# One layer of a hybrid SSM and convolution block: how the last product of the down projection gets its operands, and where the odd rows are normalised

## The chip, the core and the metric

The kernel runs on one core of a Trainium2 chip. The metric is device time in microseconds (us) for one execution; the median of three runs is given. A profile of one more execution shows each instruction of the five engines: PE (TensorE), DVE (VectorE), ACT (ScalarE), POOL (GpSimd) and SP (SyncE, which here only issues DMAs).

## What is computed

The layer takes x of 1024 rows by 1024 columns. A token-mixing half (SSM branch, short convolution, gates, output projection, LayerNorm) gives a new x. The part that matters here is the end:

```python
hid = jax.nn.silu(jnp.einsum('bsd,df->bsf', x, w_gate)) * jnp.einsum('bsd,df->bsf', x, w_up)
ffn = jnp.einsum('bsf,fd->bsd', hid, w_down)
x = layer_norm(ALPHA * x + ffn, ln2_g, ln2_b)
```

`hid` has 2816 columns, `w_down` is 2816 by 1024, and all is float32.

## The kernel before, in words

Each large product is done by Strassen's scheme: seven products of half-size matrices in place of eight. Each fp32 operand is split into a high part (rounded to `fp32r`) and a low part (what is left), and a product is three matmuls: low by high, high by low, high by high (L1480 to L1482). ACT makes the high part by a copy; DVE makes the low part by a subtraction (both through line L115, the helper `sub`).

There are two ways to split. `split` has ACT write the high part to SBUF once, and DVE subtract that from the raw tile: both inputs of DVE lie in SBUF. `psplit` has ACT write the high part twice, first to one of two PSUM banks (`hp`), then to SBUF, and DVE subtracts the PSUM copy: one input of DVE is in SBUF and one in PSUM.

The down projection runs the seven products in the order 2, 6, 3, 1, 4, 7, 5 (`ORD_E`), each in 11 steps over the inner dimension (`kp` 0 to 10), so that step n of 0 to 76 is a product and a kp: product 4 is steps 44 to 54, product 7 is steps 55 to 65, product 5, the last, is steps 66 to 76. In a usual step PE does 12 matmuls of 128 by 512 (four row blocks `tp`, three matmuls each). In the last product only `tp` 0 (and `tp` 1, three steps behind, `LAG`) run inside the steps: 3 matmuls in steps 66 to 68, then 6. After step 76 come the 9 matmuls left of `tp` 1, the 33 of `tp` 2, and 66 matmuls of 128 by 256 for `tp` 3 (L1561 to L1563).

The order of the instructions is the order in which the loop over n emits them (each engine works its own queue in that order). In step n the loop emits:

- at the first step of a product, DVE's additions of the previous product's row blocks 2 and 3 from PSUM into `acc` (`e_evac`, L112 or L1470),
- the loads for step n+8 (SP), and POOL's operand sum for step n+6 (`tB`, L106; only for products whose right operand is a sum of two blocks, so none for product 5),
- the splits for step n+3 (`e_split`): left operand A (`rAh`, `rAl`) and right operand B (`rBh`, `rBl`); in product 5 only B is left to do here, because A was split early,
- `e_early`: in the steps of the table `EARLY`, the A operand of one kp of product 5, by `psplit`; its load is issued six steps earlier,
- one stage of the generator `odd_tiles`, when it is due,
- the matmuls, and at the last step of a product the additions of row blocks 0 and 1.

`acc` holds eight row tiles. The four odd ones (`acc[:, 4 + tp]`) get their last addition from product 4, so they can be normalised while products 7 and 5 run. `odd_tiles` does that: for each of four tiles the statistics on DVE (`bn_stats` L990, `bn_aggr` L991), then one inverse square root for all four by small DVE instructions (`ln_rstd`, `ln_bias`, twelve instructions, the last at L1013), then for each half and tile `ln_half`, and the store. `ln_half` has two forms: with `engs = None` it is two DVE instructions (L1020, L1021), otherwise one activation on ACT (L1023) and a multiplication and an addition on POOL (L109, L112). The four even tiles follow after product 5: `finish` for tiles 0 to 2 (statistics on DVE, then ACT and POOL), and the last tile wholly on DVE.

Of the kernel before, what the change touches and what calls it, by code (L numbers as in the profile page):

```python
# [47 lines left out]
def kernel(  # L48
# [22 lines left out]
    V, S, G, PE = nc.vector, nc.scalar, nc.gpsimd, nc.tensor  # L71
# [52 lines left out]
    def half(h):  # L124
        return slice(512 * h, 512 * h + 512)
# [203 lines left out]
    def start(gen, s=0):  # L329
        bg.append([gen, s])  # L330
# [656 lines left out]
    def ln_stats(t, tmp_pool, mv, nm):  # L987
        stt = tmp_pool.tile([P, 2, 6], F32, tag="bst6", name=f"bn{nm}", bufs=2)
        for h in range(2):
            V.bn_stats(stt[:, h], t[:, half(h)])  # L990
        V.bn_aggr(mv, stt)  # L991

    def ln_rstd(tmp_pool, mv, n, nm):
        var = mv[:, :, 1]
        w = tmp_pool.tile([P, 5, n], F32, tag=f"lnw{n}", name=f"lnw{nm}", bufs=2)
        v, a, r, r1, b = (w[:, i] for i in range(5))
        ts(v, var, EPS, -0.5, ALU.add, ALU.mult)
        it = tmp_pool.tile([P, n], I32, tag=f"iti{n}", name=f"it{nm}", bufs=2)
        ts(it, v.bitcast(I32), -0.5, 519526879.0, ALU.mult, ALU.add)
        r0 = it.bitcast(F32)  # L1000
        for ri in (r, r1, r):
            if n == 1:
                ts(a, r0, r0, v, ALU.mult, ALU.mult)
                ts(ri, a, 1.5, r0, ALU.add, ALU.mult)
            else:
                mul(a, r0, r0)
                mul(a, a, v)
                V.scalar_tensor_tensor(ri, a, 1.5, r0, ALU.add, ALU.mult)
            r0 = ri
        return r, b  # L1010

    def ln_bias(mv, r, b):
        V.scalar_tensor_tensor(b, mv[:, :, 0], -1.0, r, ALU.mult, ALU.mult)  # L1013

    def ln_half(t, lg, mean, r, b, h, engs):
        ln_cols(t, lg, mean, r, b, half(h), engs)
# [228 lines left out]
    NK = NF // 2  # L1245
# [15 lines left out]
    def load_a(m, kp):  # L1261
        if (m, kp) not in as_:
            t = as_[m, kp] = e1a["p"].tile([P, 512], F32, tag="As", name=f"As{m}_{kp}", bufs=12)
            nc.sync.dma_start(t, a_d[m - 1, kp])
# [119 lines left out]
    def e_load(n):  # L1384
        if n < len(seq):
            m, kp = seq[n]
            if m != 5:
                load_a(m, kp)
            op = XOP[m]
            for ij in op if len(op) == 1 else op[1:]:  # L1390
                ld(kp, *ij)

    def e_add(n):
        if n < len(seq):
            m, kp = seq[n]
            op = XOP[m]
            if len(op) == 1:
                pend[n] = ld(kp, *op[0])
            else:
                pend[n] = e1.tile([P, 512], F32, tag="tB", name=f"tB{n}", bufs=4)  # L1400
                tt(pend[n], ld(kp, *op[1]), ld(kp, *op[2]), OPS[op[0]], G)

    def place(m, kp, kind):
        if m != 5:
            return (e1, f"r{kind}h", 4), (e1, f"r{kind}l", 4)
        if kind == "B":
            return (e1, f"Bx_{kp}", 1), ((e1, f"own{kp}", 1) if kp < 7 else (e1, "rBl", 4))
        if kp < 5:
            return tuple((e1a["p"], f"B00_{2 * kp + r}", 1) for r in range(2))
        return tuple((e1, f"own{2 * kp - 3 + r}", 1) for r in range(2))  # L1410

    def split_op(m, kp, kind, src):
        th, tl = place(m, kp, kind)
        h = th[0].tile([P, 512], F32R, tag=th[1], name=f"r{kind}h{m}_{kp}", bufs=th[2])
        l = tl[0].tile([P, 512], F32R, tag=tl[1], name=f"r{kind}l{m}_{kp}", bufs=tl[2])
        (split if m == 2 or (m == 5 and kind == "B") else psplit)(h, l, src)
        return [h, l]

    def e_split(n):
        if n < len(seq):  # L1420
            m, kp = seq[n]
            a = early.pop(kp) if m == 5 else split_op(m, kp, "A", as_.pop((m, kp)))
            ring[n] = a + split_op(m, kp, "B", pend.pop(n))

    early = {}
    EARLY = {40 + 2 * i: kp for i, kp in enumerate((5, 6, 7, 8, 9, 10, 0, 1, 2, 3, 4))}

    def e_early(n):
        if n + 6 in EARLY:
            load_a(5, EARLY[n + 6])  # L1430
        if n in EARLY:
            early[EARLY[n]] = split_op(5, EARLY[n], "A", as_.pop((5, EARLY[n])))

# [12 lines left out]
    def open_e2():  # L1446
        close(epi_cm)
        close(wring_cm)
        e2["cm"], e2["p"] = opened("e2")
        acc = e2["p"].tile([P, 8, D], F32, tag="acc", name="acc")  # L1450
        return acc, e2["p"].tile([P, 2, D], F32, tag="lg", name="lg2")
# [14 lines left out]
    def e_evac(m, tp):  # L1466
        for par, h, f in UPD[m]:
            t = acc[:, 4 * par + tp, half(h)]
            if (m, par, h) in ((2, 1, 0), (2, 1, 1), (3, 0, 1), (1, 0, 0)):
                V.scalar_tensor_tensor(t, t, ALPHA, eb[m, tp], ALU.mult, ALU.subtract if f is sub else ALU.add)  # L1470
            else:
                f(t, t, eb[m, tp])

    def e_mm(m, kp, tp, r):
        ah, al, bh, bl = r
        if kp == 0:
            eb[m, tp] = bank(f"pe{m}_{tp}")
        ps = eb[m, tp]
        c = slice(tp * P, (tp + 1) * P)
        PE.matmul(ps, al[:, c], bh, start=kp == 0, stop=False)  # L1480
        PE.matmul(ps, ah[:, c], bl, start=False, stop=False)  # L1481
        PE.matmul(ps, ah[:, c], bh, start=False, stop=kp == NK - 1)  # L1482

    def odd_tiles():
        mv = e2["p"].tile([P, 4, 2], F32, tag="mv4", name="mv4")
        for tp in range(4):
            ln_stats(acc[:, 4 + tp], e2["p"], mv[:, tp], f"o{tp}")
            yield 2
        r, b = ln_rstd(e2["p"], mv, 4, "o")
        ln_bias(mv, r, b)  # L1490
        yield 1
        for h in range(2):
            for tp in range(4):
                J = 4 + tp
                engs = None if h == 0 and tp < 3 else (G, G)
                ln_half(acc[:, J], lg2, mv[:, tp, 0:1], r[:, tp : tp + 1], b[:, tp : tp + 1], h, engs)
                nc.sync.dma_start(out[:, J, half(h)], acc[:, J, half(h)])
                yield 1

    LAG = 3  # L1500
    for n in range(len(seq)):
        m, kp = seq[n]
        if n == NFIRST:
            acc, lg2 = open_e2()
        if kp == 0 and n:
            for tp in (2, 3):
                e_evac(seq[n - 1][0], tp)
        e_load(n + 8)
        e_add(n + 6)
        e_split(n + 3)  # L1510
        if NFIRST <= n < NFIRST + 4:
            nc.sync.dma_start(acc[:, n - NFIRST + 4], x1_d[n - NFIRST + 4])
        if 14 <= n < 18:
            nc.sync.dma_start(acc[:, n - 14], x1_d[n - 14])
        if n == 20:
            nc.sync.dma_start(lg2, ln[:, 2:4])
        e_early(n)
        if n == 5 * NK + 3:
            start(odd_tiles(), n)
        for it in list(bg):  # L1520
            if it[1] <= n:
                try:
                    it[1] = n + next(it[0])
                except StopIteration:
                    bg.remove(it)
        if m == 5:
            e_mm(m, kp, 0, ring[n])
            if kp >= LAG:
                e_mm(m, kp - LAG, 1, ring[n - LAG])
        elif kp > 1 or n < 2:  # L1530
            for tp in range(4):
                e_mm(m, kp, tp, ring[n])
        else:
            for tp in range(2):
                e_mm(m, kp, tp, ring[n])
            if kp == 1:
                for k in range(2):
                    for tp in range(2, 4):
                        e_mm(m, k, tp, ring[n - 1 + k])
        if m != 5 and kp != 0:  # L1540
            ring.pop(n)
            if kp == 1:
                ring.pop(n - 1)
        if kp == NK - 1 and m != 5:
            for tp in range(2):
                e_evac(m, tp)
# [112 lines left out]
```

## Time and profile before

| | us |
|---|---|
| median of 3 runs | 1295.02 (1293.82 to 1295.74) |
| the profiled execution | 1294.12 |
| its span, first to last instruction | 1292.3 |
| PE busy in the span | 1207.6 (93%) |
| DVE busy | 860.5 (67%) |
| POOL busy | 783.4 (61%) |
| ACT busy | 737.0 (57%) |

The profiled execution lasted 1.8 us longer than its span and was 0.9 us below the median. All times below are us from the start of the span. A row of a timeline reads: start, duration, engine, line, operation, output<-inputs, shapes, count, and in brackets how long the engine sat idle before it and what released it. Durations overlap a little where an engine pipelines, so the pace of a queue is read from start to start. PEclk is the share of TensorE's full clock that was granted.

### The profile page before, as it was taken

To read this page: it belongs to the slowest core of one execution; us is meant where nothing else is said; L and a number is where in the kernel's file an instruction comes from. 1 tells how busy PE (TensorE), PEld (TensorE's weight loads), DVE (VectorE), ACT (ScalarE), POOL (GpSimd) and SP (SyncE) were. 2 spreads that over 40 slices of the span, in tenths; PEclk is the share of its full clock that TensorE was granted. 3 is DMA by queue.
4 is the path that set the end of the run, shared out by engine and by line. 5 is a ranking of instruction groups with operands and counts; after the bars stand their busy time and mean duration, and the time that the engine had idled before them with its cause. 6 is when DMAs were issued, how large, how long until landed. Compare 5 with 4: busy or idle time off the path is not lost. (4 is left out here: it accounts for less than half of the span.)

```text
span 1292.3 us, 16665 instructions
## 1 busy us (share of the span) xinstructions
PE 1207.6 (93%) x5365; PEld 981.3 (76%) x5365; DVE 860.5 (67%) x1319; ACT 737.0 (57%) x1288; POOL 783.4 (61%) x579
## 2 busy tenths in 40 slices
PE   7789899989899999999869999999999999999976
PEld 4577677777677888888757888888888887888756
DVE  6998688786676675688984444444344467667797
ACT  5645776778776252243433555555555555878841
POOL 4836878796862125123688777778778764544444
PEclk9989999999999999999989999999999999999988
DMA  5221343344446645224204423323222419845212
GB/s 198 74 94 46 103 117 97 116 153 144 141 140 223 204 139 199 79 98 147 98 33 145 165 82 114 106 91 122 107 98 98 155 66 348 296 135 171 70 54 77
DMA packets 88023, 166.07 MB, mean 129 GB/s; under 512 B 17792, under 2 KB 27008, under 8 KB 87680
## 3 DMA queue, kind: packets, MB, share of 16 engines
q1 hardware_dynamic: 87936, 165.00, 38.2%
q8 instruction: 43, 0.70, 0.2%
q14 instruction: 44, 0.36, 0.1%
HBM read 114.77 MB, written 44.83 MB: 123 GB/s over the span
## 5 line engine op out<-in xcount | busy, mean ns | idle before, releaser
L180 PE MATMUL ps_f<-x1h,wl_f 128*128 128x512 f32 x616 | 242.5, 394 | 13.1 <-DVE wl_f L115 9.5
L181 PE MATMUL ps_f<-x1l,wh_f 128*128 128x512 f32 x616 | 241.6, 392 | 2.8 <-DVE x1l L115 2.8
L182 PE MATMUL ps_f<-x1h,wh_f 128*128 128x512 f32 x616 | 241.3, 392 | 0.0
L115 DVE TENSOR_TENSOR wl_f<-t_f,hp 128x512 fp32r<-128x512 f32 x92 | 63.3, 688 | 166.0 <-ACT hp L137 166.0
L180 PEld LDWEIGHTS ps_f<-x1h,wl_f 128*128 128x128 f32 x616 | 116.7, 190 | 39.7 <-issue 8.5
L137 ACT ACTIVATE hp<-t_f 128x512 fp32r<-128x512 f32 x92 | 55.4, 602 | 148.7 <-POOL t_f L106 147.8
L181 PEld LDWEIGHTS ps_f<-x1l,wh_f 128*128 128x128 f32 x616 | 116.7, 189 | 27.7 <-DVE x1l L115 3.6
L182 PEld LDWEIGHTS ps_f<-x1h,wh_f 128*128 128x128 f32 x616 | 116.6, 189 | 24.3
L1481 PE MATMUL pe<-rBl,rAh 128*128 128x512 f32 x297 | 117.7, 396 | 8.8 <-DVE rBl L115 8.8
L106 POOL TENSOR_TENSOR tB<-B,B 128x512 f32<-128x512 f32 x55 | 71.3, 1296 | 83.1 <-DVE rBl L115 47.6
L1480 PE MATMUL pe<-rBh,rAl 128*128 128x512 f32 x297 | 117.6, 396 | 1.5 <-DVE acc L112 1.3
L1482 PE MATMUL pe<-rBh,rAh 128*128 128x512 f32 x297 | 116.9, 394 | 0.0
L180 PE MATMUL ps_gt<-xh,wl_gt 128*128 128x512 f32 x224 | 90.0, 402 | 5.4 <-ACT ea_gt L227 2.4
L182 PE MATMUL ps_gt<-xh,wh_gt 128*128 128x512 f32 x224 | 88.3, 394 | 0.0
L181 PE MATMUL ps_gt<-xl,wh_gt 128*128 128x512 f32 x224 | 87.7, 392 | 0.0
L106 POOL TENSOR_TENSOR t_f<-raw_f,raw_f 128x512 f32<-128x512 f32 x62 | 83.3, 1344 | 4.1 <-DVE wl_f L115 4.1
L1481 PEld LDWEIGHTS pe<-rBl,rAh 128*128 128x128 f32 x297 | 56.4, 190 | 23.8 <-DVE rBl L115 12.4
L1480 PEld LDWEIGHTS pe<-rBh,rAl 128*128 128x128 f32 x297 | 56.5, 190 | 14.9 <-DVE acc L112 2.1
L1482 PEld LDWEIGHTS pe<-rBh,rAh 128*128 128x128 f32 x297 | 56.5, 190 | 11.6
L106 POOL TENSOR_TENSOR t_f<-raw_f 128x512 f32<-128x512 f32 x43 | 57.2, 1340 | 10.2 <-DMA raw_f<-in_wgu 9.6
L109 POOL TENSOR_TENSOR hid<-sgf,ec_f 128x512 f32<-128x512 f32 x21 | 27.5, 1309 | 55.0 <-DVE sgf L109 31.8
L115 DVE TENSOR_TENSOR rAl<-As,hp 128x512 fp32r<-128x512 f32 x66 | 45.3, 687 | 20.7 <-ACT hp L137 14.9
(406 smaller groups left out, 3283.7 us busy)
## 6 DMA issues: line engine op xcount, KB each, us to landing
raw_f<-in_wgu SPq DMA_DIRECT2D x45, 512.0 KB, 3.9
As<-a_d SPq DMA_DIRECT2D x77, 256.0 KB, 3.5
a_d<-hs SPq DMA_DIRECT2D x55, 256.0 KB, 2.0
B<-in_wd SPq DMA_DIRECT2D x44, 256.0 KB, 5.3
raw_gt<-in_w SPq DMA_DIRECT2D x16, 512.0 KB, 4.5
s_d<-sg SPq DMA_DIRECT2D x32, 256.0 KB, 2.6
sgd<-s_d SPq DMA_DIRECT2D x16, 512.0 KB, 3.6
a_d<-hid SPq DMA_DIRECT2D x22, 256.0 KB, 2.2
```

The costliest lines, as they stand in the source:

```text
L106: eng.tensor_tensor(o, a, b, op)
L109: eng.tensor_tensor(o, a, b, ALU.mult)
L115: eng.tensor_tensor(o, a, b, ALU.subtract)
L137: S.activation(hp, raw, AF.Copy)
L180: PE.matmul(ps, self.lo[:, k, :], xh[:, k, :], start=first and k == 0, stop=False, skip_group_check=True)
L181: PE.matmul(ps, self.hi[:, k, :], xl[:, k, :], start=False, stop=False, skip_group_check=True)
L182: PE.matmul(ps, self.hi[:, k, :], xh[:, k, :], start=False, stop=last and k == 3, skip_group_check=True)
L1480: PE.matmul(ps, al[:, c], bh, start=kp == 0, stop=False)
L1481: PE.matmul(ps, ah[:, c], bl, start=False, stop=False)
L1482: PE.matmul(ps, ah[:, c], bh, start=False, stop=kp == NK - 1)
```

## The change

Four edits, all in the down projection:

- `split_op` takes `psplit` for the B operands of product 5 too; of the splits through it only those of product 2 keep `split`.
- `EARLY` begins at step 36 in place of 40: each early A split of product 5, and its load, is emitted four steps sooner (steps 36 to 56, every second step).
- `odd_tiles` starts at step 56 in place of 58 and takes one step for each tile's statistics in place of two: statistics in steps 56 to 59, the inverse square root in step 60, the eight `ln_half` in steps 61 to 68 (before: 58 to 64, 66, 67 to 74).
- all eight `ln_half` of the odd tiles take ACT and POOL (before, three took DVE alone).

```diff
@@ -1413,7 +1413,7 @@
-        (split if m == 2 or (m == 5 and kind == "B") else psplit)(h, l, src)
+        (split if m == 2 else psplit)(h, l, src)
@@ -1423,7 +1423,7 @@
-    EARLY = {40 + 2 * i: kp for i, kp in enumerate((5, 6, 7, 8, 9, 10, 0, 1, 2, 3, 4))}
+    EARLY = {36 + 2 * i: kp for i, kp in enumerate((5, 6, 7, 8, 9, 10, 0, 1, 2, 3, 4))}
@@ -1485,14 +1485,14 @@
             ln_stats(acc[:, 4 + tp], e2["p"], mv[:, tp], f"o{tp}")
-            yield 2
+            yield 1
...
-                engs = None if h == 0 and tp < 3 else (G, G)
+                engs = (G, G)
@@ -1515,7 +1515,7 @@
-        if n == 5 * NK + 3:
+        if n == 5 * NK + 1:
             start(odd_tiles(), n)
```

## Rows read from the trace of the kernel before

**Rows 1.** Windows of the last product: length, busy by engine, PEclk, DMA share, GB/s.
```profile
1238.27:1250.00 11.73, 7.83 (x29) 4.96 (x27) 11.28 (x22) 5.20 (x8) 6.02 (x4) 0.94 0.07 24
1250.00:1262.09 12.09, 7.34 (x18) 5.04 (x19) 11.57 (x8) 0.00 (x0) 10.21 (x7) 0.64 0.41 152
1262.09:1282.32 20.23, 20.23 (x120) 17.93 (x118) 15.27 (x46) 4.57 (x6) 11.78 (x10) 0.99 0.14 53
```
**Rows 2.** Timeline of PE, last product: first matmul, waits, last matmul.
```profile
1238.27 0.39 PE L1480 MATMUL pe<-rBh,rAl 128*128 128x512 f32 x1
...
1240.31 0.39 PE L1480 MATMUL pe<-rBh,rAl 128*128 128x512 f32 x1
...
1243.56 0.50 PE L1481 MATMUL pe<-rBl,rAh 128*128 128x512 f32 x1 [1.19 <-DVE rBl L115]
...
1247.60 0.50 PE L1481 MATMUL pe<-rBl,rAh 128*128 128x512 f32 x1 [2.38 <-DVE rBl L115]
...
1252.64 0.80 PE L1481 MATMUL pe<-rBl,rAh 128*128 128x512 f32 x1 [2.96 <-DVE rBl L115]
...
1257.68 0.50 PE L1481 MATMUL pe<-rBl,rAh 128*128 128x512 f32 x1 [2.11 <-DVE rBl L115]
...
1282.04 0.28 PE L1563 MATMUL pe<-rBh,rAh 128*128 128x256 f32 x1
```
**Rows 3.** Timeline of DVE: subtractions for product 5, alone and beside POOL.
```profile
1242.82 0.68 DVE L115 TENSOR_TENSOR rBl<-B,rBh 128x512 fp32r<-128x512 f32 x1
...
1245.79 1.75 DVE L115 TENSOR_TENSOR rBl<-B,rBh 128x512 fp32r<-128x512 f32 x1
```
**Rows 4.** Groups by line, 1238.27 to 1262.1: busy, mean ns, idle before.
```profile
L1021 DVE SCALAR_TENSOR_TENSOR acc<-acc,lnwo,lg 128x512 f32<-128x512 f32 x3 | 5.0, 1651 | 0.1
```
**Rows 5.** Timeline of POOL: operand sum, odd-tile work, first and last of `finish`.
```profile
1195.76 1.29 POOL L106 TENSOR_TENSOR tB<-B,B 128x512 f32<-128x512 f32 x1 [1.83 <-DVE rBl L115]
...
1246.96 1.73 POOL L109 TENSOR_TENSOR acc<-acc,lg 128x512 f32<-128x512 f32 x1
...
1270.15 1.29 POOL L109 TENSOR_TENSOR acc<-acc,lg 128x512 f32<-128x512 f32 x1 [9.70 <-ACT acc L1023]
...
1284.58 1.26 POOL L112 TENSOR_TENSOR acc<-acc,lg 128x512 f32<-128x512 f32 x1
```
**Rows 6.** Timeline of DVE: subtraction from PSUM, additions, statistics, inverse root, last tile.
```profile
1195.97 0.69 DVE L115 TENSOR_TENSOR rAl<-As,hp 128x512 fp32r<-128x512 f32 x1 [0.35 <-ACT hp L137]
...
1209.09 4.86 DVE L112 TENSOR_TENSOR acc<-acc,pe 128x512 f32<-128x512 f32 x8
...
1217.29 0.69 DVE L115 TENSOR_TENSOR rAl<-As,hp 128x512 fp32r<-128x512 f32 x1 [0.35 <-ACT hp L137]
...
1223.11 1.28 DVE L990 BATCH_NORM_STATS2 bno<-acc 128x6 f32<-128x512 f32 x2
1224.42 0.21 DVE L991 BATCH_NORM_AGGREGATE mv<-bno 128x2 f32<-128x12 f32 x1
...
1240.58 0.16 DVE L118 TENSOR_SCALAR lnwo<-mv 128x4 f32<-128x4 f32 x1
...
1286.35 0.74 DVE L1020 SCALAR_TENSOR_TENSOR acc<-acc,mvlast,lg 128x512 f32<-128x512 f32 x1
```
**Rows 7.** Timeline of ACT: copies of psplit, then of split, then activations.
```profile
1176.86 0.63 ACT L138 ACTIVATE rAh<-As 128x512 fp32r<-128x512 f32 x1 [0.15 <-PE pe L1482]
...
1195.35 0.59 ACT L137 ACTIVATE hp<-As 128x512 fp32r<-128x512 f32 x1
...
1232.81 4.26 ACT L121 ACTIVATE rBh<-B 128x512 fp32r<-128x512 f32 x8
...
1246.63 1.51 ACT L1023 ACTIVATE acc<-acc,lnwo 128x512 f32<-128x512 f32 x2
```
**Rows 8.** DMA issues, part 6 of the page: loads of A, us to landing.
```profile
As<-a_d SPq DMA_DIRECT2D x77, 256.0 KB, 3.5
```
**Rows 9.** Timeline of PE: the wait at the start of product 7.
```profile
1210.42 0.50 PE L1480 MATMUL pe<-rBh,rAl 128*128 128x512 f32 x1 [1.02 <-DVE acc L112]
```

## The prediction

> **What bounds the kernel now.** I read the chain that ended last first: through products 7 and 5 it runs over ACT's copies and DVE's subtractions, and passes to PE only inside product 5. Then PE's waits and the windows of that product. PE reaches product 5 at 1238.27, and nine matmuls later stands at 1240.31 [rows 2]: 2.04 / 9 = 0.227 us a matmul. The two windows up to 1262.09 hold 47 matmul rows, one of which lies in both; 46 x 0.227 = 10.4 us would do, and they took 23.8 [rows 1]. So **13.4 us** are lost. 1.19 + 2.38 + 2.96 + 2.11 = 8.6 us of it are four waits, each released by DVE's `rBl` [rows 2]; the other 4.8 are matmuls at TensorE's lower level: the granted clock is 0.94 and then 0.64 of full, against 0.99 after 1262.09 [rows 1]. From there PE runs without a gap to its last matmul at 1282.04 [rows 2], so what product 5 gains before 1262 reaches the end whole, if the tail keeps its shape.
>
> Why is `rBl` late? Alone, the subtraction with both inputs in SBUF takes 0.68; beside POOL's normalisation it takes 1.75 [rows 3], and POOL's own instruction takes 1.73 [rows 5]. In between DVE does six normalising instructions of its own, 1.65 each [rows 4]. DVE is busy 22.85 of 23.8 us there, while ACT idles [rows 1]. DVE, waiting on POOL, is the bound of this stage.
>
> **The change, part by part.**
>
> *B of product 5 through PSUM.* The subtraction that reads `hp` took 0.69 with POOL's sum of 1.29 running beside it [rows 5, 6]; neither is stretched. So I take 0.69 (queue pace 0.60, from the eight additions in 4.86 [rows 6]) for each of the 11. Bounds: 0.60 to 1.75 [rows 3]. It costs 11 more copies on ACT, 4.26 / 8 = 0.53 each [rows 7]. From the start of a copy into `hp` to the end of its subtraction passes 1195.97 + 0.69 - 1195.35 = 1.31 us [rows 6, 7].
>
> *All eight `ln_half` on ACT and POOL.* This removes six DVE instructions, some 9 us of DVE's time. It adds three activations on ACT (eight now, at 0.70 to 0.75 of pace, 1.51 for two [rows 7]) and six POOL instructions (16 now). With no DVE instruction of two SBUF inputs beside them these should take 1.29 (as the sum and `finish` do [rows 5]), not 1.73: 16 x 1.3 = 20.8 us, upper bound 16 x 1.73 = 27.7.
>
> *Statistics in steps 56 to 60.* This moves DVE work into product 7: 1.44 to 1.5 for each of four tiles, and 1242.82 - 1240.58 = 2.24 for the inverse root [rows 3, 6]. I followed DVE's queue from the early subtraction at 1217.29, at 0.60 a subtraction. The first statistics end at 1219.35. Steps 57 to 59 each bring two subtractions and a tile, 2.64 us, against PE's 12 x 0.227 = 2.72. Step 60 brings two subtractions and the root, 3.44. So `rBl` of steps 60 to 64 ends at 1220.6, 1223.3, 1225.9, 1228.6 and 1232.0. PE, counted back from 1238.27 in steps of 2.72, wants them 0.23 after 1222.0, 1224.7, 1227.4, 1230.1 and 1232.8: **margins of 1.6 down to 1.0 us**, and 1.8 for step 65. This part costs nothing while those margins hold; if they were gone, up to 4 x 1.44 + 2.24 = 8.0 us.
>
> *Early A splits four steps sooner.* Two splits (2 copies each on ACT, 4 x 0.53 = 2.1 us; two subtractions) go from steps 58 and 60, where DVE now has statistics, to steps 36 and 38. ACT has room there: in the steps before 44 it waits for PE to free its ring (still 0.15 at 1176.86 [rows 7]). Following its queue from step 36 at 0.52 a copy, it comes to step 44 about 0.35 late. That delays the additions at the product's turn, and PE's wait of 1.02 on those additions at the next turn [rows 9] grows by it: **-0.35**. Bounds: 0 (ring slack takes all) to 2.1. The loads move four steps ahead on SP's queue; they are issued six steps, 16 us, before use and land in 3.5 [rows 8], and SP has nothing to wait for but free `As` buffers. The blocks of B for product 4 stand behind them on that queue and get their turn up to two steps, 5.4 us, later; the load of a step is emitted two steps ahead of the sum that reads it, and SP runs ahead of that. I take nothing; bounds 0 to 5.4.
>
> *Product 5 then.* ACT's first activation can start at about 1230.9, when the root is done. Step 61 brings one after its four copies, step 62 four copies and one, and from step 63 each brings two copies and an activation, 1.76 us. The copy into `hp` for step 66 starts near 1234.35, for 67 to 72 1.76 apart, and from there 1.05 apart, since step 68 has the last activation. `rBl` follows 1.31 later: 1235.65 for step 66, 1239.2 for 68, 1246.2 for 72, 1250.35 for 76. PE at full pace wants `rBl` at 1238.5, 1239.9, 1244.6 and 1250.1. On DVE four additions of product 7 (4 x 0.60) come between `rBl` of steps 68 and 69, so that of 69 ends at 1242.15 against 1240.55: 1.6 late. Step 72 is 1.6 late too, the same shift and not a second one; the last is within it. So **1.6 us** of the 13.4 stay, by two queues that agree. One wait of that size was borne at full clock (after the 1.19 at 1243.56 the matmuls kept 0.5 and less; the window up to 1250 shows 0.94 [rows 1, 2]), so I add nothing for the clock.
>
> *POOL and the tail.* POOL starts on the odd tiles near 1231.7 and is done by 1252.5. `finish` wants it first at 1270.15 [rows 5], less the gain 1258.7: room of 6 us. The tail keeps its shape, 1292.3 - 1282.3 = 10 us.
>
> Sum: 13.4 - 1.6 - 0.35 = 11.4 us (0.9%). Against the profiled execution's own time 1294.12 - 11.4 = 1282.7; the median of the runs lies 0.9 above that execution, so **1283.6**.
>
> **The rivals.**
>
> *A. The clock falls again.* PE's pieces in steps 66 to 75 are short, with waits between. The two low stretches of before cost 4.8 us together, some 2.4 for each fall, and the first came after the waits of 1.19 and 2.38 [rows 2]. If ACT's queue runs 1 us slower than counted, the wait grows to 2.6 and one fall comes with it: +1.0 + 2.4 gives 1287; two falls, 1289. For it: 1.6 is between the 1.19 that was borne and the sum that was not. Against: it comes as one wait, and from then PE is fed at its own pace. [...]
>
> *B. POOL reaches the tail late.* If the 16 instructions take 1.73 still, POOL is done at 1231.7 + 27.7 = 1259.4, 0.7 after `finish` wants it. POOL's last instruction ended at 1285.84 before, 0.5 ahead of the last tile's first DVE instruction at 1286.35 [rows 5, 6], which has two SBUF inputs; past that margin two or three of the six DVE instructions there stretch from 0.74 towards 1.65 [rows 4, 6]: +2 to 3, 1286. Against: nothing in the odd tiles' stretch is left that stretched POOL. The Trainium skill ("SBUF — State Buffer", section "Who interferes with whom") states such a wait as a lock: a DVE instruction with two SBUF inputs and a GpSimd instruction that reads SBUF hold each other off for the whole instruction. By that, each meeting in the tail would cost up to POOL's 1.26 [rows 5]; the 1.75 of [rows 3] agrees.
>
> *C. The subtraction through PSUM is stretched all the same* (the change does not do what it says). Then 11 x 1.75 on DVE: `rBl` of step 76 ends near 1241.5 + 8 x 1.75 = 1255.5, 5.4 late, with a fall of the clock: 13.4 - 5.4 - 2.4 - 0.35 = 5.2 gained, 1290. Against: the 0.69 beside POOL.
>
> *D. Slower: the work lands on PE in product 7.* Place: steps 57 to 65. ACT copies into two `hp` banks in turn, and DVE frees them, so a DVE held by statistics stops ACT as well, for B and A alike. If the margins of 1.0 to 1.6 are not there, the 8.0 us of statistics and root come out as PE waits, the eight activations (8 x 0.72 = 5.8) delay the copies for steps 66 on by as much, and one fall of the clock (2.4) joins: 16.2 against 13.4, or 2.8 + 0.35 slower, 1298. It decides from the point where `rBl` of step 60 ends later than 1222.2. Against: DVE's queue of before ran 4 us ahead of PE by step 65, and half the added work fits into that.
>
> **How the numbers follow.** Forecast 1283.6 (its own range 1281.5 to 1285.5): 0.60. A 0.17, B 0.08, C 0.05, D 0.05; 0.05 for D with only some 80% of its price, which is no change. About 0.2%, 2.6 us, can be told from no change here. Faster: 0.60 + 0.17 + 0.08 + 0.05 = 0.90; same 0.05; slower 0.05. No stall at all in product 5 would give 1294.12 + 0.9 - 13.4 = 1281.6, less some tenths if the wait at the turn shrinks: low 1281. The top takes in A with two falls: 1289.
>
> **What would show it.** Right: PE enters product 5 near 1238.6; its waits in it sum to about 1.6, most of it at step 69; the granted clock stays near 1; each `rBl` takes 0.69 from `hp`; POOL's `acc` instructions take 1.3 and end before 1254; the last matmul starts near 1270.6. Wrong: PE waits on `rAl` or `rBl` in steps 57 to 65; `rBl` near 1.7; POOL still busy with odd tiles when the first `finish` activation ends; waits on DMA for `B` or `As`; or a gain in product 5 that the tail gives back.

## The result

The changed kernel took a median of 1283.07 us in six runs (1282.1 to 1285.14), the kernel before 1295.40 in six (1293.82 to 1296.06). The ratio is 0.9909, with a 95% interval of 0.9896 to 0.9921: 0.9% faster. The forecast was 1283.6, the range 1281 to 1289.

The profiled execution of after took 1285.0 us (span 1283.2), 9.1 less than that of before, though the last stage gained more: from the first matmul of product 2 to the end it took 1283.2 - 1058.4 = 224.8 us, before 1292.3 - 1055.6 = 236.7. That is **11.9 us less**. The other 2.8 were lost ahead of product 2, in work that the change does not touch (last section). So the traces are compared from product 2 on, and the rows of after lie some 2.75 us later than those of before at the same step.

Windows of the last product in after, from its first matmul to the first matmul of the last row block (length; busy time of PE, PEld, DVE, ACT and POOL, where PEld is PE's weight load; PEclk, DMA share, GB/s), to be read against [rows 1]:

```profile
1241.02:1250.00 8.98, 7.83 (x33) 5.90 (x32) 6.33 (x10) 8.98 (x17) 8.67 (x8) 1.00 0.29 107
1250.00:1265.21 15.21, 15.21 (x68) 12.58 (x67) 11.22 (x31) 4.44 (x9) 9.43 (x9) 1.00 0.18 67
```

DVE was busy 96% of that stretch before, and is busy 70% and 74% of the two windows now; ACT is full until 1250 and POOL nearly; the granted clock is 1.00 where it was 0.94 and 0.64. PE's waits in products 7 and 5 of after (timeline of PE, wait and releaser in brackets), against [rows 2, 9]:

```profile
1213.15 0.50 PE L1480 MATMUL pe<-rBh,rAl 128*128 128x512 f32 x1 [1.39 <-DVE acc L112]
1214.35 0.50 PE L1480 MATMUL pe<-rBh,rAl 128*128 128x512 f32 x1 [0.23 <-DVE acc L112]
1243.46 0.49 PE L1480 MATMUL pe<-rBh,rAl 128*128 128x512 f32 x1 [0.24 <-ACT rBh L138]
1244.87 0.50 PE L1481 MATMUL pe<-rBl,rAh 128*128 128x512 f32 x1 [0.91 <-DVE rBl L115]
```

These four are all: the first two stand at the start of product 7, the last two in step 69. The four waits of [rows 2] are gone; one small pair is left at step 69, where the forecast put it. None is in steps 57 to 65. The wait at the start of product 7 went from 1.02 to 1.39.

The queues behind it, DVE first, then ACT, then POOL, against [rows 3, 6], [rows 7] and [rows 5]:

```profile
1234.03 0.68 DVE L115 TENSOR_TENSOR rBl<-tB,hp 128x512 fp32r<-128x512 f32 x1
...
1237.64 0.69 DVE L115 TENSOR_TENSOR rBl<-B,hp 128x512 fp32r<-128x512 f32 x1 [1.06 <-ACT hp L137]
...
1241.74 2.47 DVE L112 TENSOR_TENSOR acc<-acc,pe 128x512 f32<-128x512 f32 x4
1244.13 1.28 DVE L115 TENSOR_TENSOR rBl<-B,hp 128x512 fp32r<-128x512 f32 x2
...
1277.33 0.74 DVE L1020 SCALAR_TENSOR_TENSOR acc<-acc,mvlast,lg 128x512 f32<-128x512 f32 x1
```

```profile
1233.51 0.82 ACT L1023 ACTIVATE acc<-acc,lnwo 128x512 f32<-128x512 f32 x1 [0.66 <-DVE lnwo L1013]
...
1237.03 0.58 ACT L137 ACTIVATE hp<-B 128x512 fp32r<-128x512 f32 x1
1237.55 0.62 ACT L138 ACTIVATE rBh<-B 128x512 fp32r<-128x512 f32 x1
1238.07 0.80 ACT L1023 ACTIVATE acc<-acc,lnwo 128x512 f32<-128x512 f32 x1
1238.77 0.58 ACT L137 ACTIVATE hp<-B 128x512 fp32r<-128x512 f32 x1
```

```profile
1234.40 1.30 POOL L109 TENSOR_TENSOR acc<-acc,lg 128x512 f32<-128x512 f32 x1 [6.99 <-ACT acc L1023]
...
1254.36 1.29 POOL L112 TENSOR_TENSOR acc<-acc,lg 128x512 f32<-128x512 f32 x1
1261.11 1.30 POOL L109 TENSOR_TENSOR acc<-acc,lg 128x512 f32<-128x512 f32 x1 [5.46 <-ACT acc L1023]
...
1275.59 1.26 POOL L112 TENSOR_TENSOR acc<-acc,lg 128x512 f32<-128x512 f32 x1
```

Each `rBl` takes 0.69 with POOL busy beside it, where it took 1.75. ACT goes round every 1.74 us (1237.03 to 1238.77). The four additions of product 7 stand between `rBl` of step 68 and the pair of steps 69 and 70. POOL's instructions take 1.3 in place of 1.73; the odd tiles are done at 1255.65, and `finish` wants POOL 5.5 us later. At the end POOL stops at 1276.85, 0.5 ahead of the last tile's first instruction of two SBUF inputs, as in before.

### The profile page after: what moved, and what is told of

Read it like the earlier page. It is cut to its first block, busy times and chain, and to the rows that moved or that the text cites. A ratio compares the mean times of both kernels' runs of the same rounds, so it can differ in the third digit from the quotient of the medians.

```text
span 1283.2 us, 16680 instructions
## 1 busy us (share of the span) xinstructions
PE 1206.2 (94%) x5365; PEld 981.1 (76%) x5365; DVE 849.8 (66%) x1313; ACT 747.4 (58%) x1302; POOL 786.2 (61%) x585
```

## The experiments

Each kernel was profiled and timed in four or more executions beside the kernel before. The columns come from the traces: the loss in product 5 is the time from its first matmul to the first 128 by 256 matmul, less the 99 x 0.2267 = 22.44 us that its 99 large matmuls need at full pace; product 7 needs 29.9 at full pace; the tail is from the last matmul's start to the end. The ratio is to executions of before taken beside each kernel (medians 1294.64 for e1 to e4, 1294.34 for e5 to e8_early_spaced, 1293.61 for the last three), so it is not the quotient with the first row.

| kernel | median us | ratio to before, 95% interval | loss in product 5 | product 7 | tail | product 2 to end |
|---|---|---|---|---|---|---|
| before | 1295.40 | | 13.53 | 31.75 | 10.26 | 236.7 |
| after | 1283.07 | 0.9909 (0.9896 to 0.9921) | 1.75 | 32.13 | 10.19 | 224.8 |
| e1_psplit_only | 1287.78 | 0.9947 (0.9931 to 0.9964) | 5.83 | 31.75 | 10.27 | 229.2 |
| e2_actpool_only | 1290.45 | 0.9967 (0.9954 to 0.9980) | 4.37 | 31.75 | 15.38 | 232.0 |
| e3_no_psplit | 1285.94 | 0.9929 (0.9914 to 0.9944) | 4.67 | 32.12 | 10.24 | 228.6 |
| e4_no_pool | 1283.53 | 0.9912 (0.9897 to 0.9926) | 3.94 | 31.75 | 10.21 | 227.4 |
| e5_late_odd | 1288.13 | 0.9948 (0.9933 to 0.9963) | 2.99 | 32.13 | 13.14 | 229.8 |
| e6_early40 | 1284.47 | 0.9922 (0.9908 to 0.9937) | 4.20 | 32.37 | 10.24 | 228.2 |
| e7_double_stats | 1289.78 | 0.9962 (0.9949 to 0.9976) | 2.69 | 36.76 | 10.27 | 231.2 |
| e8_early_spaced | 1279.07 | 0.9877 (0.9862 to 0.9892) | 0.78 | 30.01 | 10.26 | 222.4 |
| e10_changed_again | 1282.38 | 0.9912 (0.9890 to 0.9934) | 1.80 | 32.13 | 10.26 | 225.7 |
| e8_again | 1279.91 | 0.9892 (0.9874 to 0.9911) | 0.73 | 30.04 | 10.26 | 222.5 |
| e9_spaced_evac | 1278.50 | 0.9882 (0.9865 to 0.9900) | 0.00 | 30.04 | 10.26 | 221.8 |

The theory: DVE and POOL stretch each other where a DVE instruction reads two tiles of SBUF beside a POOL instruction; the split through PSUM and the move of all normalising to ACT and POOL end that, and the earlier start keeps ACT and POOL in time. The rivals: the subtractions were late only because they queued behind DVE's normalising; and, the earlier start does nothing.

**Only the split through PSUM.** The kernel before with

```diff
-        (split if m == 2 or (m == 5 and kind == "B") else psplit)(h, l, src)
+        (split if m == 2 else psplit)(h, l, src)
```

> The kernel before with one edit: the B operands of product 5 go through PSUM. Theory (the subtraction with two SBUF inputs and POOL's instructions stretch each other): every rBl takes 0.69 again, about 3.4 us less before step 69 and 3.3 less for the last four, but the three pairs of DVE normalising instructions stay in the queue and stay stretched near 1.65; PE's loss in product 5 falls from 13.4 us to 6 to 9, the time to 1288 to 1291. Rival (the subtractions are late only because they queue behind DVE's normalising): at most 1 us is gained, 1294 to 1295.

Measured 1287.78, and a loss of 5.83: both just under the lower end of the theory's ranges. `rBl` takes 0.69 throughout. DVE's own normalising (timeline of DVE) shows why it gained more than expected:

```profile
1243.76 0.74 DVE L1020 SCALAR_TENSOR_TENSOR acc<-acc,mv,lg 128x512 f32<-128x512 f32 x1
1244.54 0.75 DVE L1021 SCALAR_TENSOR_TENSOR acc<-acc,lnwo,lg 128x512 f32<-128x512 f32 x1
1245.21 0.68 DVE L115 TENSOR_TENSOR rBl<-B,hp 128x512 fp32r<-128x512 f32 x1
1245.81 1.84 DVE L1020 SCALAR_TENSOR_TENSOR acc<-acc,mv,lg 128x512 f32<-128x512 f32 x1
1247.68 1.63 DVE L1021 SCALAR_TENSOR_TENSOR acc<-acc,lnwo,lg 128x512 f32<-128x512 f32 x1
```

Two of the three pairs ran at 0.75, the third at 1.84 and 1.63: the first activations come later on ACT, behind the added copies, so POOL begins later and meets only the last pair. The rival's limit of 1 us falls.

**Only the move to ACT and POOL.** The kernel before with

```diff
-                engs = None if h == 0 and tp < 3 else (G, G)
+                engs = (G, G)
```

> The kernel before with one edit: all eight ln_half of the odd tiles on ACT and POOL, at their old steps and with the old split. Theory: DVE has only subtractions left, but each meets POOL and takes about 1.7; PE's loss in product 5 falls to 4 us, or 6 with a fall of the clock. POOL has 16 instructions of about 1.7 from 1243.8, so it works on odd tiles until near 1270, some 10 us past the time at which finish wants it; then the last tile's six DVE instructions run beside POOL and stretch. Most of the gain of product 5 is given back in the tail: 1289 to 1293. Rival (POOL has room, only DVE's own normalising matters): 1283 to 1286.

Measured 1290.45, inside the theory's range and outside the rival's. Product 5 loses 4.37 in place of 13.53, but the tail grows by 5.1 us. Timeline of DVE in that tail, the last tile:

```profile
1277.64 0.93 DVE L1020 SCALAR_TENSOR_TENSOR acc<-acc,mvlast,lg 128x512 f32<-128x512 f32 x1
1278.60 1.63 DVE L1021 SCALAR_TENSOR_TENSOR acc<-acc,lnwlast,lg 128x512 f32<-128x512 f32 x1
1280.16 1.55 DVE L1020 SCALAR_TENSOR_TENSOR acc<-acc,mvlast,lg 128x320 f32<-128x320 f32 x1
1281.74 1.43 DVE L1021 SCALAR_TENSOR_TENSOR acc<-acc,lnwlast,lg 128x320 f32<-128x320 f32 x1
1283.10 1.41 DVE L1020 SCALAR_TENSOR_TENSOR acc<-acc,mvlast,lg 128x192 f32<-128x192 f32 x1
```

The same instruction on 192 columns takes 1.41, where it takes 0.41 in the tails of before and after: it starts at 1283.10 and ends at 1284.51, just behind POOL's last instruction (1282.90 to 1284.29), so its own size hardly counts. The Trainium skill ("SBUF — State Buffer", section "Who interferes with whom") states this as an exclusive lock held for a whole instruction; the 1.41 agrees. POOL ran without a pause from 1244.30 to 1284.29. This is rival B of the prediction, with its price.

**The changed kernel without the split through PSUM** (the first diff undone).

> The changed kernel with B of product 5 split without PSUM again. Theory: POOL runs its 16 instructions beside the 11 subtractions; rBl takes about 1.7 each, the last one is 5 us late, POOL's instructions take 1.7 and end 5 us later. PE loses 5 to 8 us in product 5 in place of 1.2: 1287 to 1291. Rival (with the normalising off DVE the split no longer matters): 1283 to 1284, and ACT's shorter queue even gives some tenths back.

Measured 1285.94, between the two, nearer to the theory; the trace gives 3.8 us more than after (228.6 against 224.8). DVE and POOL, one row of each:

```profile
1241.62 12.53 DVE L115 TENSOR_TENSOR rBl<-B,rBh 128x512 fp32r<-128x512 f32 x8
```

```profile
1246.77 1.74 POOL L109 TENSOR_TENSOR acc<-acc,lg 128x512 f32<-128x512 f32 x1
```

Eight subtractions in 12.53 us, 1.57 each, and POOL at 1.74: the contention is back. It costs less than expected: the loss of 4.67 is 1.6 us of one fall of the clock (seven matmuls 0.43 to 0.59 apart) and 3.1 of waiting, 2.2 of it one wait on `rBl` at step 69; and POOL was done at 1256.7, 4.2 ahead of `finish`.

**The kernel before without POOL's part of the odd tiles.** It leaves out the multiplication and the addition of the five half tiles that go to ACT and POOL.

```diff
-                ln_half(acc[:, J], lg2, mv[:, tp, 0:1], r[:, tp : tp + 1], b[:, tp : tp + 1], h, engs)
+                if engs is None:
+                    ln_half(acc[:, J], lg2, mv[:, tp, 0:1], r[:, tp : tp + 1], b[:, tp : tp + 1], h, engs)
+                else:
+                    S.activation(acc[:, J, half(h)], acc[:, J, half(h)], AF.Identity, bias=b[:, tp : tp + 1], scale=r[:, tp : tp + 1])
```

> The kernel before with POOL's ten instructions (multiplication and addition) of five odd ln_half left out, so that those tiles come out wrong; DVE's and ACT's part stays. Theory (contention, not DVE's own work, is the larger part): DVE's six normalising instructions take 0.7 and rBl 0.6 to 0.69; PE's loss in product 5 falls from 13.4 to about 3.5, or 6 with one fall of the clock: 1284 to 1288. Rival (the normalising on DVE is the cost, whatever POOL does): at most 3 us gained, 1292 or more.

Measured 1283.53, just under the theory's range: by the medians nearly the whole gain of the change, by the traces from product 2 on 9.3 of its 11.9 us, with the split and DVE's normalising as they were. Groups by line, first the subtraction in before (1238 to 1262), then this kernel (1238 to 1255):

```profile
L115 DVE TENSOR_TENSOR rBl<-B,rBh 128x512 fp32r<-128x512 f32 x8 | 10.6, 1353 | 0.0
```

```profile
L115 DVE TENSOR_TENSOR rBl<-B,rBh 128x512 fp32r<-128x512 f32 x8 | 5.2, 685 | 0.0
...
L1021 DVE SCALAR_TENSOR_TENSOR acc<-acc,lnwo,lg 128x512 f32<-128x512 f32 x3 | 2.3, 752 | 0.1
L1020 DVE SCALAR_TENSOR_TENSOR acc<-acc,mv,lg 128x512 f32<-128x512 f32 x3 | 2.2, 745 | 0.0
```

The same DVE instructions: `rBl` took 1353 ns before and takes 685 now, L1021 took 1651 [rows 4] and takes 752. So 9.6 us (13.53 - 3.94) of the loss go when POOL's instructions do, and the rival falls. But 9.6 is not the contention's share of a sum: e2, which takes DVE's normalising away and leaves the subtractions stretched, takes 9.2 (13.53 - 4.37) off the same loss. Stretch and normalising together made DVE's queue too long; either one alone leaves a loss of about 4 us.

**The changed kernel with the odd tiles at their old steps.**

```diff
-            yield 1
+            yield 2
...
-        if n == 5 * NK + 1:
+        if n == 5 * NK + 3:
```

> The changed kernel with the odd tiles at their old steps (statistics 58 to 64, root 66, ln_half 67 to 74). Theory: ACT's eight activations now fall between the copies of steps 71 on, 1.76 us a step against PE's 1.36, and the last rBl is nearly 4 us late; POOL starts near 1244 and its 16 x 1.3 us reach to 1265, 5 us past the first activation of finish, so the tail is stretched by 2 to 3 us too: 1286 to 1290, that is 3 to 7 slower than the changed kernel. Rival (the earlier start is idle, only the split and the engines count): 1283 to 1284.

Measured 1288.13, as the theory said: 1.2 us more loss in product 5 and 2.9 in the tail. POOL's end (timeline of POOL) and the last tile (of DVE):

```profile
1279.38 1.71 POOL L109 TENSOR_TENSOR acc<-acc,lg 128x512 f32<-128x512 f32 x1
1281.16 1.59 POOL L112 TENSOR_TENSOR acc<-acc,lg 128x512 f32<-128x512 f32 x1
```

```profile
1278.28 1.69 DVE L1020 SCALAR_TENSOR_TENSOR acc<-acc,mvlast,lg 128x512 f32<-128x512 f32 x1
1280.00 1.63 DVE L1021 SCALAR_TENSOR_TENSOR acc<-acc,lnwlast,lg 128x512 f32<-128x512 f32 x1
1281.56 1.54 DVE L1020 SCALAR_TENSOR_TENSOR acc<-acc,mvlast,lg 128x320 f32<-128x320 f32 x1
```

The earlier start is what pays for POOL's six added instructions.

**The changed kernel with the early splits at their old steps** (`36 + 2 * i` to `40 + 2 * i`).

> The changed kernel with the early A splits at steps 40 to 60 again. Theory: PE's wait at the start of product 7 falls by 0.35; two subtractions and four copies come back into steps 58 and 60, where the margins were 1.0 to 1.6 us: DVE is 0.6 to 1.2 later there and ACT up to 2.1 later at the first copies for product 5. No wait of PE in steps 57 to 65 beyond 0.5 us, and the wait in product 5 grows from 1.15 to 2 or 3: in all 0.5 to 2 slower than the changed kernel. Rival (there is slack enough): 0.3 faster.

Measured 1284.47, 1.4 above after, the ranges of the runs overlapping; by the traces from product 2 on it is 2.4 to 3.4 slower (228.2 against 225.7 and 224.8), more than expected. The trace shows the exchange: the first wait at the start of product 7 is back at 1.01 (1.39 in after), but in step 64, where the forecast had its smallest margin, `rAl` ends only at 1231.62 and the matmuls fall 0.6 behind, so product 7 is 0.24 longer all the same; and ACT comes to step 69 later, 0.78 in place of 0.24. What was not expected is the clock (timeline of PE):

```profile
1240.97 0.50 PE L1480 MATMUL pe<-rBh,rAl 128*128 128x512 f32 x1 [0.78 <-ACT rBh L138]
1242.37 0.50 PE L1481 MATMUL pe<-rBl,rAh 128*128 128x512 f32 x1 [0.91 <-DVE rBl L115]
...
1243.68 0.63 PE L1482 MATMUL pe<-rBh,rAh 128*128 128x512 f32 x1
1244.10 0.63 PE L1480 MATMUL pe<-rBh,rAl 128*128 128x512 f32 x1
```

After the two waits eight matmuls are 0.43 apart, which costs 1.6 us; the granted clock there (1243.25 to 1246.24) is 0.50.

**The changed kernel with the statistics done twice** in steps 56 to 59.

```diff
             ln_stats(acc[:, 4 + tp], e2["p"], mv[:, tp], f"o{tp}")
+            ln_stats(acc[:, 4 + tp], e2["p"], mv[:, tp], f"p{tp}")
```

> The changed kernel with the statistics of each odd tile done twice in its step, 1.44 us more in each of steps 56 to 59, the second time into the same numbers. Theory: a step of DVE grows from 2.64 to 4.08 against PE's 2.72, the margins of about 1.6 us are used up in the second step, and PE waits on rAl and rBl in steps 59 to 63, about 4 us in sum; the activations start as much later, and the wait in product 5 stays or grows by 1.5; a fall of the clock may join: 1287 to 1291. Rival (DVE has free time in product 7, the statistics are hidden whatever they cost): within 1 us of the changed kernel.

Measured 1289.78. Product 7 is 4.6 us longer and product 5 loses 0.9 more. PE's waits in product 7 (timeline of PE):

```profile
1224.77 0.47 PE L1480 MATMUL pe<-rBh,rAl 128*128 128x512 f32 x1 [0.71 <-DVE rAl L115]
1228.79 0.47 PE L1480 MATMUL pe<-rBh,rAl 128*128 128x512 f32 x1 [0.68 <-DVE rAl L115]
1232.80 0.47 PE L1480 MATMUL pe<-rBh,rAl 128*128 128x512 f32 x1 [0.70 <-DVE rAl L115]
1236.29 0.47 PE L1480 MATMUL pe<-rBh,rAl 128*128 128x512 f32 x1 [0.21 <-DVE rAl L115]
```

They are on `rAl`, each at the begin of a step, in steps 61 to 64 (expected: 59 to 63). The idle times sum to 2.3; the first two matmuls after each wait come slower too, and from start to start it is the 4.6. The margin that hides the statistics in the changed kernel is real and no larger than counted: a second helping goes almost whole to PE. This is the place of rival D.

**The early splits at every third step**, `EARLY = {24 + 3 * i ...}` in the changed kernel.

> The changed kernel with the early A splits at every third step from 24 to 54. Theory (the wait at the start of product 7 is ACT's queue, full to 96% in the steps before, which lets DVE reach the additions late): ACT's load falls to 89% there, DVE reaches the additions about 2 us sooner, PE's waits of 1.39 and 0.23 at the start of product 7 shrink to 0.3 or less; product 5 as in the changed kernel: 1 to 1.6 us faster, 1281 to 1282. Rival (the additions wait for PE's own last matmuls): no difference.

Measured 1279.07, and 1279.91 beside the changed kernel's 1282.38 on one chip:

> The kernel with early A splits at every third step, beside the changed kernel on one chip. The first profile gives 222.4 us from product 2 to the end against 224.8: 2.4 us faster. If the 4.0 us between the medians of the two earlier runs were all this edit's, 4 us faster.

> The changed kernel once more, beside the two below on one chip. Expected by the trace: product 2 to the end 224.8 us as in its first profile, whatever the stages before product 2 take; they differed by up to 4.7 us between profiles of kernels that are alike there (product 2 starts at 1053.7 to 1058.4). Time 1281 to 1285.

From product 2 on the traces give 222.4 and 222.5 against 224.8 and 225.7: 2.3 to 3.3 us faster, and 2.5 by the medians on one chip, where 1 to 1.6 had been expected at first. 2.1 of it are the start of product 7 (32.13 to 30.04, no wait left) and 1.0 the wait in product 5. The expectation had counted only the first. Timeline of DVE at the turn, in after (product 7 begins at 1208.89) and in e8_early_spaced (at 1206.01):

```profile
1211.22 0.69 DVE L115 TENSOR_TENSOR rAl<-As,hp 128x512 fp32r<-128x512 f32 x1 [0.35 <-ACT hp L137]
1211.82 4.87 DVE L112 TENSOR_TENSOR acc<-acc,pe 128x512 f32<-128x512 f32 x8
```

```profile
1206.26 0.69 DVE L115 TENSOR_TENSOR rAl<-As,hp 128x512 fp32r<-128x512 f32 x1 [0.35 <-ACT hp L137]
1206.86 4.87 DVE L112 TENSOR_TENSOR acc<-acc,pe 128x512 f32<-128x512 f32 x8
```

DVE, paced by ACT's copies into `hp`, reaches the additions 2.93 us after product 7 begins in after, and 0.85 here. So the wait at the turn was ACT's queue, not PE's own end. The changed kernel came to 225.7 in its second profile, 0.9 more than expected; the difference lies between products 2 and 7, 151.3 against 150.5.

**And the additions of product 7 out of the way.** Beside the spaced splits,

```diff
-                yield 1
+                yield 4 if h == 0 and tp == 3 else 1
...
-        if kp == 0 and n:
+        if kp == 0 and n and m != 5:
             for tp in (2, 3):
                 e_evac(seq[n - 1][0], tp)
+        if m == 5 and 4 <= kp < 8:
+            e_evac(7, kp - 4)
...
-        if kp == NK - 1 and m != 5:
+        if kp == NK - 1 and m not in (5, 7):
```

> As the kernel with early A splits at every third step, and beside that the additions of product 7 put off to steps 70 to 73 and the second four activations of the odd tiles to steps 68 to 71. Theory (the wait left in product 5 is first the four additions between two subtractions, then ACT's 1.76 us a step): the loss in product 5 falls from 0.8 us to 0.4 or less, POOL ends its odd work 1 us later, still 2 us before finish wants it: 0.2 to 0.6 us faster than with the splits alone. Rival (that wait is at the floor of a handover between ACT, DVE and PE): no difference.

Measured 1278.50, the fastest; against the kernel with the spaced splits alone 1.4 by the medians, with overlapping intervals, and 0.7 by the traces. Its windows of product 7 and product 5:

```profile
1205.67:1235.71 30.04, 30.04 (x133) 24.71 (x132) 24.95 (x52) 24.46 (x45) 13.77 (x11) 1.00 0.05 18
1235.71:1258.15 22.44, 22.44 (x100) 18.59 (x99) 16.94 (x40) 12.40 (x23) 17.15 (x15) 1.00 0.22 81
```

PE is busy for the whole of both, at full clock; the loss is nil. The handover was no floor.

## Why the prediction was right

- *What bounds the kernel.* 13.4 us were said to be lost in product 5; from start to start it is 13.53. The cause named, DVE stretched by POOL, is shown: without POOL's instructions 9.6 us of it go (e4), and with the old split in the changed kernel the stretch returns (e3). With DVE's normalising out of the queue the same stretch leaves only 4.37 in product 5 (e2); it took both to make it 13.53.
- *The split through PSUM* was priced at 0.69 beside POOL and took 0.69.
- *ACT and POOL.* The copy into `hp` for step 66 was put at 1234.35, which with the shift of 2.75 is 1237.1; it started at 1237.03. `rBl` of step 69 was put at 1242.15, shifted 1244.9; it ended at 1244.81. POOL's end was put at 1252.5, shifted 1255.25; it was 1255.65.
- *What stays in product 5* was put at 1.6 us and is 1.75, at the step and by the two queues named: the wait on DVE goes with the additions, a smaller one on ACT's `rBh` stands ahead of it. e9 takes both away and shows that nothing else was hidden there.
- *Statistics in product 7* were called free by margins of 1.0 to 1.8. `rBl` of step 64 ended at 1234.71, and PE wanted it at 1235.8: 1.1. No wait came, and e7 shows where the cover ends. One reading beside it was wrong: the prediction's argument against rival D gave DVE's queue of before a lead of 4 us at step 65; there `rBl` ended at 1233.07 and PE wanted it at 1235.8, a lead of 2.7.
- *The early splits* were priced at -0.35 and cost 1.39 - 1.02 = 0.37 at the turn. What they bring was told only as room for DVE; e6 shows the amount on the other side: 0.6 at step 64, 0.54 more of ACT's wait at step 69, and a fall of the clock that may follow.
- *The tail* kept its shape, 10.2 us, and POOL's last instruction the same 0.5 us ahead of DVE's. e2 and e5 show that rival B was the one to watch: without the earlier start it costs 3 to 5 us.

One term was mis-sized without harm to the sum: the lower clock. I put 4.8 us of before to it, 2.4 a fall. From start to start the four waits are 9.8 us, not 8.6, so at most 3.7 are left for two stretches, and a fall measured by itself (e3, e6) costs 1.6. Rival A was dearer on paper than it is. The sum itself held: product 5 gained 11.78 (13.53 - 1.75) and product 7 lost 0.38 (32.13 - 31.75), which is the 11.4 forecast. That the median agrees by half a microsecond is in part luck: executions of one kernel differ by 3 us.

## What to carry to other kernels

When a vector instruction is slow in one stage only, look for what the GpSimd runs beside it: here a subtraction of two tiles in SBUF took 0.68 alone and 1.75 beside the GpSimd, and 0.69 beside it with one operand in PSUM. Two delays in one queue can cost far more together than either alone (e2, e4). Moving work to the GpSimd pays only if it also starts early enough to be gone before the next stage with two-operand vector work; otherwise the same contention comes back in the tail (e2, e5). Before moving work into a stage that has slack, count that slack in the queue, step by step; here 1 us of margin carried the change, and the same work once more went to TensorE almost whole.

## What the runs showed of the hardware that was not expected

- **A fall of TensorE's clock does not follow from the waits alone.** The waits of 0.78 and 0.91 in e6 were followed by eight matmuls 0.43 apart, and one wait of 2.02 in e3 by seven; the same 0.78 and 0.91 in e7 were not, nor the 0.24 and 0.91 of after, nor four waits of 1.21, 0.39, 0.40 and 0.40 in e4, nor 1.18, 0.39, 0.39 and 2.36 in e1, where the granted clock is 1.00 over the whole of product 5. What decides is not settled by these runs.
- **Stages that no edit touches move the total by some us.** The first matmul of product 2 starts between 1053.7 (e1) and 1058.4 (after) in the thirteen profiles; the changed kernel itself started it at 1058.4 once and at 1054.7 the other time (e10). Part of it is seen in the granted clock ahead: in the window 400 to 454 it is 1.00 in before and 0.97 in after. Where one edit is worth 1 us, the traces compared from product 2 on told more than the medians.
